# Gates, branch projections and merge computed with tokens on partitions and 512 weight columns moving, merged columns transposed afterwards

## The chip, the cores and the metric

The kernel runs on one core of one Trainium2 chip. The metric is the device time of one execution in microseconds (us). All arrays are float32 in memory. TensorE (PE in the profile) multiplies, VectorE (DVE) and ScalarE (ACT) prepare operands and empty PSUM, SyncE (SP) issues nearly all weight DMAs in the order of the program, GpSimd (POOL) issues a few small ones.

## What is computed

One transformer layer over 256 latent tokens with 256 context tokens and D_MODEL = 2048. The change touches the gates and the merge of its two branches:

```python
proj = h @ w_in[l]                       # h: 256 x 2048; columns: q, kv, u, v, gates
attn_o = _attention(q, k, v)             # 256 x 1024
sgu_o = _sgu(u, v, ...)                  # 256 x 1024
g = sigmoid(proj[..., OFF_GATE:])        # 256 x 4096
merged = g[..., :2048] * (attn_o @ w_br_attn) + g[..., 2048:] * (sgu_o @ w_br_sgu)
x_new = x + g1 * (merged @ w_out[l])
...                                      # then norm, modulation and a SwiGLU FFN
```

## The kernel before

**Products.** A float32 weight tile of 128 x 512 is split into a high part `whi` (ACT, L241) and a low part `wlo` (DVE, L242); activations are kept as high and low halves of one 128 x 512 tile (`split_to`, L290 on ACT and L291 on DVE). A product is three matmuls (`mm3`): high x high, high x low, low x high. There are two ways round. With **channels on partitions** the 128 x 128 weight tile is stationary and the 256 tokens move (`mm<-g,whi` in the profile). With **tokens on partitions** a 128 x 128 activation tile is stationary and 512 weight columns move (`mm<-whi,g`). `mm_wides` is a form of the first way: both halves of the activation move as 512 columns past `whi`, then the high half as 256 columns past `wlo`; the two halves of the PSUM bank are added afterwards (L641, L642).

**Stages.** In order: modulation vectors and the input projection in chunks of the contraction (`in_chunk`, order given by the string `ORDER`, with blocks "T" of 512 columns, tokens on partitions, and tiles "F" of 128 columns, channels on partitions); the spatial-gating branch; query, key and value up-projections; attention; branch projections and merge; output projection (`project(mg, wout, ...)`); norm; FFN. The gate columns are PE work that fills other stages: `fill_items` is a generator that yields after every 1 MB of weights, and `SGU_GATES`, `UQ_GATES` and `ATT_GATES` say how many steps are placed after which piece. What is left of it (two steps and the eight steps of the projection of the spatial branch) runs after the attention (`fill(40, MOD_RATE)`). Then the loop over `wbra` projects the attention output, multiplies by the gate (L872), adds the other branch (L873) and splits the result into the tiles `mg` (L290, L291), channels on partitions, as `project` needs them.

**Beside it.** `background(rate)` places modulation work between the steps: each item loads 512 KB of `w_mod` and adds it to an accumulator on DVE (L427); 96 items must be done before the last column block of the output projection. Raw weights have 10 buffers of 512 KB, `whi` and `wlo` 8 each, which is two 1 MB steps ahead of PE. PSUM has 4 banks `mm` and 4 `ax`. A scheduler puts the instructions of each engine in one fixed row; each engine then runs its row in order.

Of the kernel before, what the change touches and what calls it, by code (L numbers as in the profile page):

```python
# [9 lines left out]
F32R = mybir.dt.float32r  # L10
AF = mybir.ActivationFunctionType
ALU = mybir.AluOpType

P = 128
D = 2048
KT = D // P
# [17 lines left out]
OFF_KVC = Q_LORA  # L34
# [31 lines left out]
HOLD_AT = 0  # L66


NB_Q, NB_V = 1, 2
NB_T = NB_Q + NB_V  # L70
NT_U, NT_G = 8, 32
KV_COLS = KV_LORA + ROPE

NT_GE = 4
NT_F = NT_U + NT_GE

ATT_GATES = [2, 2, 2, 2, 0, 4, 0, 2]
UQ_GATES = [2, 2, 0, 0, 0, 0]
# [44 lines left out]
def block_kernel(  # L123
# [43 lines left out]
    def slot(dt=F32):  # L167
        return gp.tile([P, 512], dt, tag="g", name=f"g{uid()}")
# [4 lines left out]
    def mmbank():  # L173
        return pm.tile([P, 512], F32, tag="mm", name=f"mm{uid()}")
# [76 lines left out]
    def flat(ap, off, ncols):  # L251
        return ap[off:off + P * ncols]
# [40 lines left out]
    def hilo(t):  # L293
        return t[:, 0:256], t[:, 256:512]
# [316 lines left out]
    for o in ORDER:  # L611
        todo[o].pop(0)()

    acc_v = acc_t[NB_Q:]
    acc_u = acc[0:NT_U // 2]


    gate_a, gate_b = acc[NT_U // 2:], []
    sgo = []
    raw_gates = list(gate_a)  # L620

    def sigmoids():

# [1 line left out]
            S.activation(d, d, AF.Sigmoid)  # L625
        raw_gates.clear()

    def fill_items():
        for i in range((NT_G - NT_GE) // 2):
            d = slot()  # L630
            pair = [mmbank(), mmbank()]
            for c in range(2):
                w = W(flat(wgate, (2 * i + c) * P * WCOLS, WCOLS), WCOLS)
                for kk in range(KT // 2):
                    k = c * (KT // 2) + kk
                    mm_wides(pair, [w.cols((2 * kk + h) * P) for h in range(2)], hs[k], k == 0, k == KT - 1)
                if c == 0:
                    yield
            for h, ps in enumerate(pair):
                v = d[:, h * 256:(h + 1) * 256]  # L640
                S.activation(v, ps[:, 256:512], AF.Copy)  # L641
                V.tensor_tensor(out=v, in0=ps[:, 0:256], in1=v, op=ALU.add)  # L642
            raw_gates.append(d)
            (gate_b if i < NT_G // 4 else gate_a).append(d)
            yield

        sigmoids()
        for i in range(8):
            w = W(flat(wbrs, i * P * WCOLS, WCOLS), WCOLS)
            ps = mmbank()  # L650
            for j in range(2):
                for k in range(8):
                    mm3(ps[:, j * 256:(j + 1) * 256], w.cols((j * 8 + k) * P), hilo(sgo[k]), k == 0, k == 7)
            V.tensor_tensor(out=gate_b[i], in0=ps, in1=gate_b[i], op=ALU.mult)
            yield

    gi = fill_items()
# [205 lines left out]


    mg = []
    for i in range(8):
        w = W(flat(wbra, i * P * WCOLS, WCOLS), WCOLS)
        ps = mmbank()
        for j in range(2):
            for k in range(8):  # L870
# [3 lines left out]
        for j in range(2):  # L874
# [171 lines left out]
def _layout(inp):  # L1046
# [44 lines left out]
    for ang in (row, col):  # L1091
# [19 lines left out]
    ge = OFF_GATE + NT_GE * P  # L1111
    wg = np.concatenate([wi[:, OFF_GATE + D:], wi[:, ge:OFF_GATE + D]], axis=1)
    wg = wg.reshape(2, KT // 2, P, (NT_G - NT_GE) // 2, 2, P)
    o["wgate"] = np.concatenate([
        x for i in range((NT_G - NT_GE) // 2) for c in range(2) for x in _chunk(wg[c, :, :, i].transpose(1, 0, 2, 3))])
    blocks = np.concatenate([wi[:, :OFF_KVC], wi[:, OFF_V:OFF_GATE]], axis=1).reshape(KT, P, NB_T, 512)
    tiles = np.concatenate([wi[:, OFF_U:OFF_V], wi[:, OFF_GATE:ge]], axis=1).reshape(KT, P, NT_F, P)
    a = {"T": blocks, "F": tiles}
    o["win"] = np.concatenate([
        x for g, items in in_chunks() for x in _chunk(np.concatenate(  # L1120
# [13 lines left out]
        inp["b_spatial"][0].reshape(-1)]).reshape(-1, 512))  # L1134
    o["xN"] = np.ascontiguousarray(inp["x"][0])

    pairs = [[2 * i, 2 * i + 1] for i in range(8)]
    o["wbrs"] = _pack(inp["w_br_sgu"][0], list(range(8)), pairs)
    o["wbra"] = _pack(inp["w_br_attn"][0], list(range(8)), pairs)
# [32 lines left out]
```

## Time and profile before

| | before |
|---|---|
| median of 3 runs (lowest, highest) | 1431.43 us (1430.92, 1431.45) |
| the profiled execution's own time | 1432.35 us |
| its span, first to last instruction | 1430.5 us |
| mean granted TensorE clock | 0.997 |
| PE busy | 1403.3 us (98%) |
| DVE busy | 1009.4 us (71%) |
| ACT busy | 766.0 us (54%) |

The stages in the trace: input projection to about 220 us, spatial branch and up-projections with gates to 350, attention with gates to 487, the last gates to 498, the spatial branch's projection to 550, the attention branch's to 597, the output projection to 681, then the FFN. A busy PE row counts the pipeline's length too, so the duration of one matmul is longer than the step from its start to the next one's; where the cost of a stream of matmuls is wanted, the steps between starts are to be read.

### The profile page before, as it was taken

The page shows a single profiled execution, that of the slowest core. Times are in us where ns is not written, and L with a number is a line of the kernel's source. Part 1 is how long each engine was busy: PE and PEld are TensorE (multiplying, and loading weights), DVE is VectorE, ACT ScalarE, POOL GpSimd, SP SyncE. Part 2 cuts the span into 40 slices and gives each one's busy share as a digit, 9 for nine tenths or more (in the row PEclk, how much of TensorE's full clock was granted, in tenths as well). Part 3 has the DMA queues.
Part 4 walks back from the last instruction along what each step waited for, and adds up shares of the span by engine and source line. Part 5 has one row for each costly group of instructions (what it writes and reads, how often), then busy time and mean ns, then how long its engine had stood idle before and what let it go on. Part 6 is the DMA issues. An engine that isn't in the chain of part 4 may idle for free.

```text
span 1430.5 us, 23109 instructions
## 1 busy us (share of the span) xinstructions
PE 1403.3 (98%) x8390; PEld 1187.3 (83%) x8390; DVE 1009.4 (71%) x1748; ACT 766.0 (54%) x1438; POOL 21.9 (2%) x44
## 2 busy tenths in 40 slices
PE   6999999999999999999999999999999999999998
PEld 3787899896777799987888888888888888888887
DVE  2677687985798688999766666666666667786553
ACT  4655466565544745554666555555555554444442
POOL 0000000001100000000000000000000000000000
PEclk9999999999999999999999999999999999999999
DMA  9987876674698598898444555555555568898560
GB/s 370 359 316 294 342 277 237 241 275 146 208 355 321 166 408 294 289 402 341 161 162 153 187 191 191 186 190 187 189 191 188 192 209 303 310 374 301 197 206 32
DMA packets 104020, 355.50 MB, mean 249 GB/s; under 512 B 12504, under 2 KB 14936, under 8 KB 103904
## 3 DMA queue, kind: packets, MB, share of 16 engines
q1 hardware_dynamic: 101952, 350.30, 67.5%
q0 software_dynamic: 1952, 3.72, 1.0%
q8 instruction: 66, 1.08, 0.3%
q14 instruction: 50, 0.41, 0.1%
HBM read 351.83 MB, written 2.13 MB: 247 GB/s over the span
## 4 chain that ended last, share of the span: by engine, by line
PE 86%; DVE 6%; DMA 5%; issue 2%; ACT 2%; SPq 0%; POOL 0%; DVEq 0%; ACTq 0%; POOLq 0%
PE mm L255 80%; PE ax L255 5%; DVE wlo L242 2%; DVE acc L427 2%; DMA raw<-in_wmod_dram 1%; DMA raw<-in_win_dram 1%; DMA raw<-in_wout_dram 1%; PE ax L840 1%; DMA g<-in_rows_dram 0%; ACT whi L241 0%; DMA m_d<-g 0%; DMA sh<-m_d 0%; DVE g L837 0%; ACT g L386 0%; DMA g<-in_xT_dram 0%
## 5 line engine op out<-in xcount | busy, mean ns | idle before, releaser
L241 ACT ACTIVATE whi<-raw 128x512 fp32r<-128x512 f32 (+1 forms) x900 | 555.4, 627 | 481.8 <-PE mm L255 334.8
L242 DVE TENSOR_TENSOR wlo<-raw,whi 128x512 fp32r<-128x512 f32 (+1 forms) x900 | 603.8, 685 | 263.5 <-ACT whi L241 255.1
L255 PE MATMUL mm<-g,whi 128*128 128x512 f32 (+1 forms) x2880 | 767.9, 357 | 0.0
L255 PE MATMUL mm<-g,wlo 128*128 128x256 f32 x2368 | 505.3, 281 | 0.0
L255 PEld LDWEIGHTS mm<-g,wlo 128*128 128x128 f32 x2368 | 438.3, 189 | 78.9 <-issue 2.0
L255 PEld LDWEIGHTS mm<-g,whi 128*128 128x128 f32 x2880 | 447.9, 190 | 14.6 <-issue 8.3
L255 PE MATMUL mm<-whi,g 128*128 128x512 f32 (+1 forms) x1312 | 401.3, 385 | 1.9 <-ACT whi L241 1.2
L255 PEld LDWEIGHTS mm<-whi,g 128*128 128x128 f32 x1312 | 244.6, 189 | 53.9 <-issue 3.7
L255 PE MATMUL mm<-wlo,g 128*128 128x512 f32 (+1 forms) x656 | 251.5, 384 | 0.7 <-DVE wlo L242 0.7
L427 DVE SCALAR_TENSOR_TENSOR acc<-raw,silw,acc 128x1024 f32<-128x1024 f32 x120 | 153.4, 1279 | 20.3 <-DMA raw<-in_wmod_dram 19.7
L255 PEld LDWEIGHTS mm<-wlo,g 128*128 128x128 f32 x656 | 123.7, 189 | 25.7 <-DVE wlo L242 2.5
L561 DVE TENSOR_TENSOR g<-mm,g 128x512 f32<-128x512 f32 (+1 forms) x72 | 46.3, 654 | 23.4 <-PE mm L255 22.9
L290 ACT ACTIVATE g<-g 128x256 fp32r<-128x256 f32 x100 | 39.1, 412 | 13.9 <-DVE g L1008 8.3
L1006 DVE TENSOR_TENSOR g<-mm,g 128x256 f32<-128x256 f32 x88 | 33.3, 420 | 17.4 <-ACT g L1005 17.3
L1005 ACT ACTIVATE g<-mm 128x256 f32<-128x256 f32 x88 | 29.0, 381 | 30.9 <-PE mm L255 30.9
L291 DVE TENSOR_TENSOR g<-g,g 128x256 fp32r<-128x256 f32 x100 | 40.2, 420 | 7.1 <-ACT g L290 7.0
L255 PE MATMUL ax<-g,g 128*128 128x128 f32 (+2 forms) x224 | 42.7, 374 | 0.2 <-DVE g L702 0.2
L255 PEld LDWEIGHTS ax<-g,g 128*128 128x128 f32 (+1 forms) x224 | 26.7, 190 | 11.7 <-issue 9.2
L255 PE MATMUL ax<-raw,silw 128*32 128x256 f32 (+1 forms) x576 | 31.6, 358 | 3.7 <-DMA raw<-in_wmod_dram 3.6
L255 PEld LDWEIGHTS ax<-raw,silw 128*32 128x32 f32 x576 | 17.0, 109 | 16.3 <-DMA raw<-in_wmod_dram 5.7
L386 ACT ACTIVATE g<-g,m 128x256 f32<-128x256 f32 x32 | 17.6, 593 | 10.2 <-DVE m L375 5.8
L835 ACT ACTIVATE g<-g,nb,rq 128x512 f32<-128x512 f32 x16 | 13.0, 811 | 14.4 <-DVE nb L833 14.3
(146 smaller groups left out, 452.0 us busy)
## 6 DMA issues: line engine op xcount, KB each, us to landing
raw<-in_wmod_dram SPq DMA_DIRECT2D x192, 512.0 KB, 6.6
raw<-in_wffi_dram SPq DMA_DIRECT2D x176, 512.0 KB, 3.2
raw<-in_wffo_dram SPq DMA_DIRECT2D x88, 512.0 KB, 4.8
raw<-in_wgate_dram SPq DMA_DIRECT2D x56, 512.0 KB, 5.0
raw<-in_win_dram SPq DMA_DIRECT2D x48, 512.0 KB, 7.0
raw<-in_wout_dram SPq DMA_DIRECT2D x32, 512.0 KB, 7.6
raw<-in_wbrs_dram SPq DMA_DIRECT2D x16, 512.0 KB, 9.0
raw<-in_wbra_dram SPq DMA_DIRECT2D x16, 512.0 KB, 6.4
```

What stands on the lines that cost most here:

```text
L241: S.activation(hi[:, :e], raw[:, q:q + e], AF.Copy)
L242: V.tensor_tensor(out=lo[:, :e], in0=raw[:, q:q + e], in1=hi[:, :e].bitcast(F32), op=ALU.subtract)
L255: nc.tensor.matmul(out, lhsT, rhs, start=start, stop=stop)
L290: S.activation(dst_hi, src, AF.Copy)
L291: V.tensor_tensor(out=dst_lo, in0=src, in1=dst_hi.bitcast(F32), op=ALU.subtract)
L386: S.activation(v, v, AF.Identity, bias=m[:, 2 * jj + s:2 * jj + s + 1], scale=m[:, 2 * n + 2 * jj + s:2 * n + 1 + 2 * jj + s])
L427: V.scalar_tensor_tensor(out=acc, in0=w.raw[0], scalar=sil[:, k, 0:1], in1=acc, op0=ALU.mult, op1=ALU.add)
L561: V.tensor_tensor(out=d, in0=ps, in1=d, op=ALU.add)
L835: exp = S.activation(t, t, AF.Exp, bias=nb, scale=rq[:, col:col + 1], accum_out=sm)
L840: nc.tensor.transpose(tp[:, k * P:(k + 1) * P], t[:, k * P:(k + 1) * P], ident)
L1005: S.activation(d, ps[:, 256:512], AF.Copy)
L1006: V.tensor_tensor(out=d, in0=ps[:, 0:256], in1=d, op=ALU.add)
```

## The change

All 32 tiles of gate columns become 8 blocks of 512 columns with tokens on partitions: one in the input projection (a fourth "T" block in place of four "F" tiles), seven in `fill_items`. A block needs two PSUM banks, one for each 128 tokens, and four 1 MB steps (`quarter`), where a pair of tiles needed two banks and two steps. Both branch projections are done the same way, four blocks of two steps. The merged values now have tokens on partitions, so after each block of the attention branch eight 128 x 128 transposes on PE (L884) turn them, and `split_to` reads the turned columns from PSUM. Weights are laid out anew on the host; bytes and counts of DMAs stay.

```diff
-        for i in range((NT_G - NT_GE) // 2):
-            d = slot()
-            pair = [mmbank(), mmbank()]
...
-                    mm_wides(pair, [w.cols((2 * kk + h) * P) for h in range(2)], hs[k], k == 0, k == KT - 1)
...
-                S.activation(v, ps[:, 256:512], AF.Copy)
-                V.tensor_tensor(out=v, in0=ps[:, 0:256], in1=v, op=ALU.add)
+    def quarter(ps, src, w_d, i, c, nk):
+        w = W(flat(w_d, i * P * WCOLS, WCOLS), WCOLS)
+        for j in range(4):
+            k = 4 * c + j
+            for tt in range(2):
+                mm3(ps[tt], rows_of(src, k, tt), w.cols(j * 512, 512), k == 0, k == nk - 1)
...
+        for i in range(NB_G - NB_GE):
+            ps = [mmbank(), mmbank()]
+            for c in range(KT // 4):
+                quarter(ps, hs, wgate, i * (KT // 4) + c, c, KT)
...
+            for tt in range(2):
+                S.activation(d[tt], ps[tt], AF.Copy)
...
-        for i in range(8):
...
-                    mm3(ps[:, j * 256:(j + 1) * 256], w.cols((j * 8 + k) * P), hilo(sgo[k]), k == 0, k == 7)
-            V.tensor_tensor(out=gate_b[i], in0=ps, in1=gate_b[i], op=ALU.mult)
+        for i in range(4):
+            ps = [mmbank(), mmbank()]
+            for c in range(2):
+                quarter(ps, sgo, wbrs, 2 * i + c, c, 8)
...
     mg = []
-    for i in range(8):
...
-                mm3(ps[:, j * 256:(j + 1) * 256], w.cols((j * 8 + k) * P), hilo(ao[k]), k == 0, k == 7)
-        V.tensor_tensor(out=gate_a[i], in0=ps, in1=gate_a[i], op=ALU.mult)
-        V.tensor_tensor(out=gate_a[i], in0=gate_a[i], in1=gate_b[i], op=ALU.add)
-        for j in range(2):
-            t = slot(F32R)
-            split_to(t[:, 0:256], t[:, 256:512], gate_a[i][:, j * 256:(j + 1) * 256])
-            mg.append(t)
-        background(MOD_RATE)
+    for i in range(4):
+        ps = [mmbank(), mmbank()]
+        for c in range(2):
+            quarter(ps, ao, wbra, 2 * i + c, c, 8)
+            background(MOD_RATE)
+        for tt in range(2):
+            g = gate_a[i][tt]
+            V.tensor_tensor(out=g, in0=ps[tt], in1=g, op=ALU.mult)
+            V.tensor_tensor(out=g, in0=g, in1=gate_b[i][tt], op=ALU.add)
+        for j in range(0, 4, 2):
+            tp = auxbank()
+            for jj in range(2):
+                for tt in range(2):
+                    nc.tensor.transpose(tp[:, jj * 256 + tt * P:jj * 256 + (tt + 1) * P],
+                                        gate_a[i][tt][:, (j + jj) * P:(j + jj + 1) * P], ident)
+            for jj in range(2):
+                t = slot(F32R)
+                split_to(t[:, 0:256], t[:, 256:512], tp[:, jj * 256:(jj + 1) * 256])
+                mg.append(t)
```

PE's row before, where the third item of the `wbra` loop follows the second (`mm_6400` and `mm_6484` are their PSUM banks, `g_...` the activations):

```order
L255 MATMUL mm_6400<-g_5518,wlo_6397 128x256
L255 MATMUL mm_6400<-g_5530,whi_6396 128x256 x2
L255 MATMUL mm_6400<-g_5530,wlo_6397 128x256
L255 MATMUL mm_6484<-g_4537,whi_6466 128x256 x2
L255 MATMUL mm_6484<-g_4537,wlo_6467 128x256
L255 MATMUL mm_6484<-g_4549,whi_6466 128x256 x2
```

PE's row now, where the second block follows the first (`mm_5858` and `mm_5859` are the second block's banks, `g_167` and `g_168` the first block's merged values of tokens 0 to 127 and 128 to 255, `ax_...` the banks of the transposes):

```order
L255 MATMUL mm_5859<-whi_5862,g_4281 128x512
L255 MATMUL mm_5858<-whi_5866,g_4293 128x512
L884 MATMUL ax_5836<-cst,g_167 128x128
L884 MATMUL ax_5847<-cst,g_167 128x128
L255 MATMUL mm_5858<-wlo_5867,g_4293 128x512
L255 MATMUL mm_5858<-whi_5866,g_4293 128x512
L884 MATMUL ax_5836<-cst,g_168 128x128
L884 MATMUL ax_5836<-cst,g_167 128x128
L884 MATMUL ax_5836<-cst,g_168 128x128
L884 MATMUL ax_5847<-cst,g_168 128x128
L884 MATMUL ax_5847<-cst,g_167 128x128
L884 MATMUL ax_5847<-cst,g_168 128x128
```

PE's row had nothing between two items that needs DVE's merge; now the merged values of the block just finished are read after seven matmuls of the next block (ten after the third and the fourth block).

DVE's row before, around the multiplication of the third item:

```order
L242 TENSOR_TENSOR wlo_6631<-raw_6624,whi_6630 128x512
L872 TENSOR_TENSOR g_4594<-mm_6484,g_4594 128x512
L242 TENSOR_TENSOR wlo_6637<-raw_6634,whi_6636 128x512
L873 TENSOR_TENSOR g_4594<-g_4594,g_3108 128x512
L242 TENSOR_TENSOR wlo_6641<-raw_6634,whi_6640 128x512
L291 TENSOR_TENSOR g_6535<-g_4594,g_6535 128x256
```

DVE's row now, after the first block:

```order
L242 TENSOR_TENSOR wlo_5910<-raw_5907,whi_5909 128x512
L427 SCALAR_TENSOR_TENSOR acc_5825<-raw_5904,silw,acc_5825 128x1024
L242 TENSOR_TENSOR wlo_5914<-raw_5907,whi_5913 128x512
L877 TENSOR_TENSOR g_167<-mm_5716,g_167 128x512
L877 TENSOR_TENSOR g_168<-mm_5717,g_168 128x512
L878 TENSOR_TENSOR g_167<-g_167,g_2926 128x512
L878 TENSOR_TENSOR g_168<-g_168,g_2927 128x512
L242 TENSOR_TENSOR wlo_5920<-raw_5917,whi_5919 128x512
L242 TENSOR_TENSOR wlo_5924<-raw_5917,whi_5923 128x512
L291 TENSOR_TENSOR g_5841<-ax_5836,g_5841 128x256
```

The four multiplications and additions of a block stand together, behind an accumulation (L427) and the split of weights, and the splits of the merged values come after PE's transposes. In front of the fourth block's four stand the two additions of a bias row (L413), which wait for a DMA of `in_rows`.

## Rows read from the trace of the kernel before

**Rows 1.** The page: busy time of each engine, and PE's busy tenths in 40 slices.
```profile
PE 1403.3 (98%) x8390; PEld 1187.3 (83%) x8390; DVE 1009.4 (71%) x1748; ACT 766.0 (54%) x1438; POOL 21.9 (2%) x44
PE   6999999999999999999999999999999999999998
```

**Rows 2.** PE's waits: who waited for whom, us in total, times, longest.
```profile
PE ax L840 <- DVE g L837: 4.8, 10, 1.2
...
PE mm L255 <- DVE wlo L242: 0.7, 2, 0.6
```

**Rows 3.** Busy time by stretch: stretch, length, each engine, clock, DMA share, GB/s.
```profile
120.00:220.00 100.00, 99.41 (x764) 87.04 (x763) 76.10 (x162) 56.66 (x119) 0.00 (x0) 1.00 0.76 286
400.00:487.00 87.00, 83.58 (x482) 63.33 (x481) 69.04 (x127) 46.61 (x93) 5.90 (x11) 1.00 0.74 267
498.00:550.00 52.00, 52.00 (x440) 51.76 (x439) 41.88 (x59) 23.56 (x40) 0.00 (x0) 1.00 0.96 378
550.00:597.00 47.00, 47.00 (x372) 45.62 (x365) 44.81 (x71) 24.81 (x49) 3.06 (x6) 1.00 0.85 297
597.00:660.00 63.00, 63.00 (x281) 50.89 (x280) 62.79 (x87) 31.19 (x57) 3.06 (x6) 1.00 0.99 379
```

**Rows 4.** The chain that ended last, 545 to 720 us (start, us, what).
```profile
579.40 0.03 DVE g L872
...
586.00 6.96 DMA g<-in_rows_dram
...
628.82 7.43 DMA raw<-in_wout_dram
...
668.88 12.10 PE mm L255 x52
```

**Rows 5.** PE's timeline, a pair of gate tiles (start, us, what, count).
```profile
488.76 0.63 PE L255 MATMUL mm<-g,whi 128*128 128x512 f32 x2
...
489.23 0.39 PE L255 MATMUL mm<-g,wlo 128*128 128x256 f32 x2
...
489.46 0.63 PE L255 MATMUL mm<-g,whi 128*128 128x512 f32 x2
```

**Rows 6.** PE's timeline, projection of the spatial branch.
```profile
499.25 0.40 PE L255 MATMUL mm<-g,whi 128*128 128x256 f32 x2
...
499.61 0.40 PE L255 MATMUL mm<-g,whi 128*128 128x256 f32 x2
```

**Rows 7.** PE's timeline, output projection.
```profile
597.32 0.62 PE L255 MATMUL mm<-whi,g 128*128 128x512 f32 x2
...
598.00 0.62 PE L255 MATMUL mm<-whi,g 128*128 128x512 f32 x2
```

**Rows 8.** PE's timeline, eight transposes of the query latents amid matmuls.
```profile
205.26 1.11 PE L512 MATMUL ax<-cst,g 128*128 128x128 f32 x8
206.13 0.47 PE L255 MATMUL mm<-whi,g 128*128 128x512 f32 x1
206.44 0.40 PE L255 MATMUL mm<-wlo,g 128*128 128x512 f32 x1
```

**Rows 9.** Groups of instructions by form: count, busy us, mean ns of one, idle before.
```profile
L840 PE MATMUL ax<-cst,g 128*128 128x128 f32 x64 | 10.1, 281 | 5.0 <-DVE g L837 4.8
```

**Rows 10.** DVE's timeline, attention branch's projection.
```profile
584.28 1.27 DVE L427 SCALAR_TENSOR_TENSOR acc<-raw,silw,acc 128x1024 f32<-128x1024 f32 x1
585.48 0.68 DVE L872 TENSOR_TENSOR g<-mm,g 128x512 f32<-128x512 f32 x1
...
587.88 0.75 DVE L291 TENSOR_TENSOR g<-g,g 128x256 fp32r<-128x256 f32 x2
588.55 1.28 DVE L242 TENSOR_TENSOR wlo<-raw,whi 128x512 fp32r<-128x512 f32 x2
589.76 1.27 DVE L427 SCALAR_TENSOR_TENSOR acc<-raw,silw,acc 128x1024 f32<-128x1024 f32 x1
593.05 1.36 DVE L413 TENSOR_TENSOR g<-g,g 128x512 f32<-128x512 f32 x2 [2.02 <-DMA g<-in_rows_dram]
```

More of the change, by code (lines that the diff above doesn't have):

```diff
@@ L66 @@
 HOLD_AT = 0
-NB_Q, NB_V = 1, 2
-NB_T = NB_Q + NB_V
-NT_U, NT_G = 8, 32
+NB_Q, NB_V, NB_G = 1, 2, 8
+NT_U = 8
 KV_COLS = KV_LORA + ROPE
-NT_GE = 4
-NT_F = NT_U + NT_GE
+NB_GE = 1
+NB_T = NB_Q + NB_V + NB_GE
+NT_F = NT_U
 ATT_GATES = [2, 2, 2, 2, 0, 4, 0, 2]
@@ L612, in block_kernel @@
         todo[o].pop(0)()
-    acc_v = acc_t[NB_Q:]
+    acc_v = acc_t[NB_Q:NB_Q + NB_V]
     acc_u = acc[0:NT_U // 2]
-    gate_a, gate_b = acc[NT_U // 2:], []
+    gate_a, gate_b = acc_t[NB_Q + NB_V:], []
     sgo = []
-    raw_gates = list(gate_a)
+    raw_gates = [t for g in gate_a for t in g]
     def sigmoids():
@@ L626, in sigmoids @@
         raw_gates.clear()
-    def fill_items():
-        for i in range((NT_G - NT_GE) // 2):
-            d = slot()
-            pair = [mmbank(), mmbank()]
+    def quarter(ps, src, w_d, i, c, nk):
[4 more added lines that the diff above has]
+                mm3(ps[tt], rows_of(src, k, tt), w.cols(j * 512, 512), k == 0, k == nk - 1)
+    def fill_items():
+        for i in range(NB_G - NB_GE):
+            ps = [mmbank(), mmbank()]
+            for c in range(KT // 4):
+                quarter(ps, hs, wgate, i * (KT // 4) + c, c, KT)
+                if c < KT // 4 - 1:
+                    yield
+            d = [slot(), slot()]
+            for tt in range(2):
+                S.activation(d[tt], ps[tt], AF.Copy)
+            raw_gates.extend(d)
+            (gate_b if i < NB_G // 2 else gate_a).append(d)
+            yield
+        sigmoids()
+        for i in range(4):
+            ps = [mmbank(), mmbank()]
             for c in range(2):
-                w = W(flat(wgate, (2 * i + c) * P * WCOLS, WCOLS), WCOLS)
-                for kk in range(KT // 2):
-                    k = c * (KT // 2) + kk
-                    mm_wides(pair, [w.cols((2 * kk + h) * P) for h in range(2)], hs[k], k == 0, k == KT - 1)
+                quarter(ps, sgo, wbrs, 2 * i + c, c, 8)
                 if c == 0:
                     yield
-            for h, ps in enumerate(pair):
-                v = d[:, h * 256:(h + 1) * 256]
-                S.activation(v, ps[:, 256:512], AF.Copy)
-                V.tensor_tensor(out=v, in0=ps[:, 0:256], in1=v, op=ALU.add)
[L643 to L647, printed above, removed]
-        for i in range(8):
-            w = W(flat(wbrs, i * P * WCOLS, WCOLS), WCOLS)
-            ps = mmbank()
-            for j in range(2):
-                for k in range(8):
-                    mm3(ps[:, j * 256:(j + 1) * 256], w.cols((j * 8 + k) * P), hilo(sgo[k]), k == 0, k == 7)
-            V.tensor_tensor(out=gate_b[i], in0=ps, in1=gate_b[i], op=ALU.mult)
+            for tt in range(2):
+                V.tensor_tensor(out=gate_b[i][tt], in0=ps[tt], in1=gate_b[i][tt], op=ALU.mult)
             yield
@@ L865, in block_kernel @@
     mg = []
-    for i in range(8):
[L867 to L870, printed above, removed]
-                mm3(ps[:, j * 256:(j + 1) * 256], w.cols((j * 8 + k) * P), hilo(ao[k]), k == 0, k == 7)
-        V.tensor_tensor(out=gate_a[i], in0=ps, in1=gate_a[i], op=ALU.mult)
-        V.tensor_tensor(out=gate_a[i], in0=gate_a[i], in1=gate_b[i], op=ALU.add)
-        for j in range(2):
-            t = slot(F32R)
-            split_to(t[:, 0:256], t[:, 256:512], gate_a[i][:, j * 256:(j + 1) * 256])
-            mg.append(t)
-        background(MOD_RATE)
+    for i in range(4):
[10 more added lines that the diff above has]
+            for jj in range(2):
+                for tt in range(2):
+                    nc.tensor.transpose(tp[:, jj * 256 + tt * P:jj * 256 + (tt + 1) * P],
[4 more added lines that the diff above has]
+                mg.append(t)
     def project(src, w_d, cb, nk, rate, last=1):
@@ L1110, in _layout @@
     o["wkv"] = np.concatenate([x for ks in kv_groups() for x in _chunk(kv[ks].transpose(1, 0, 2), 3 * KV_COLS)])
[L1111 to L1117, printed above, removed]
+    ge = OFF_GATE + NB_GE * 512
+    o["wgate"] = _nat(np.concatenate([wi[:, OFF_GATE + D:], wi[:, ge:OFF_GATE + D]], axis=1))
+    blocks = np.concatenate([wi[:, :OFF_KVC], wi[:, OFF_V:ge]], axis=1).reshape(KT, P, NB_T, 512)
+    tiles = wi[:, OFF_U:OFF_V].reshape(KT, P, NT_F, P)
     a = {"T": blocks, "F": tiles}
@@ L1135, in _layout @@
     o["xN"] = np.ascontiguousarray(inp["x"][0])
-    pairs = [[2 * i, 2 * i + 1] for i in range(8)]
-    o["wbrs"] = _pack(inp["w_br_sgu"][0], list(range(8)), pairs)
-    o["wbra"] = _pack(inp["w_br_attn"][0], list(range(8)), pairs)
+    o["wbrs"] = _nat(inp["w_br_sgu"][0])
+    o["wbra"] = _nat(inp["w_br_attn"][0])
     o["wout"] = _nat(inp["w_out"][0])
```

## The prediction

> **What bounds the kernel now.** I read the busy times and the 40 slices first. PE is busy 98% of the span, and only the first and the last slice are below nine tenths [rows 1], so the engine to watch is PE, and what the change is worth is first of all what PE's own stream becomes shorter by. A busy share can hide short stalls, so I read next PE's list of waits: the largest item is 4.8 us in the attention, where transposes wait for the softmax, and waits for a split weight come to 0.7 us in all [rows 2]. Then the stretches [rows 3]: from 498 to 660 us PE is busy all the time, but there two others come close. DVE is busy 44.81 of 47 us in the projection of the attention branch and 62.79 of 63 in the output projection, and the DMA engines run at a share of 0.96 and 0.99 around it. The chain that ended last says the same: from 579.40 to 668.88 us it doesn't run over PE but over DVE and DMAs (a bias row from `in_rows`, 6.96 us; a piece of `w_out`, 7.43 us), and PE comes back only at 668.88 [rows 4]. So before 550 us PE alone sets the pace; from there to 669 us PE and DVE with the DMAs are tied.
>
> **What a stream of matmuls costs.** Steps between starts, not durations. One pair of gate tiles (256 weight columns) for one k takes 489.46 - 488.76 = 0.70 us for four matmuls [rows 5], so 1.40 us for 512 columns and one k. Channels on partitions with `mm3` take 499.61 - 499.25 = 0.36 us for 128 columns [rows 6], so 1.44 us for 512. Tokens on partitions take 598.00 - 597.32 = 0.68 us for 512 columns and 128 tokens [rows 7], so 1.36 us for all 256, or 0.2267 us for a matmul. The moving columns are the same, 3072, in all three; there are 8, 12 and 6 matmuls for them, and what is saved is what each matmul costs beside its columns.
>
> **The change part by part.**
> Gates in `fill_items`: 7 blocks x 16 k x (1.40 - 1.36) = 4.5 us less on PE. Half of it lies among the attention, where PE is busy 83.58 of 87 us [rows 3] and fills gaps of the softmax; there a shorter filler may leave a longer gap. I take 4.0, with 2.2 (all of the attention's half lost) and 4.5 as ends. DVE and ACT lose the additions of the two PSUM halves, which is no part of the sum, since PE sets the pace there.
> Gate block in the input projection: 16 k x (1.44 - 1.36) = 1.3 us. The last two of six groups of k (8 of 16) lie where PE is busy 99.41 of 100 us [rows 3] and count fully, 0.6 us; the earlier ones lie partly where PE waits for data. I take 0.9, ends 0.6 and 1.3.
> Projection of the spatial branch: 4 blocks x 8 k x 0.08 = 2.6 us. That stretch has the DMA engines at 0.96 [rows 3], but PE is 52.00 of 52 there: two steps of split weights cover it. If the cover is gone the 2.6 us are lost.
> Projection of the attention branch: the same 2.6 us.
> Transposes: 4 blocks x 8 = 32. Eight of them took 206.13 - 205.26 = 0.87 us amid such matmuls, and the matmul behind them took 0.31 instead of 0.23 to its successor [rows 8], so 0.95 us for eight and 3.8 us for 32. The ends are 32 x 0.109 = 3.5 and, if every one cost its whole duration of 0.281 [rows 9], 32 x 0.281 = 9.0. I take 3.8, since these rows stand between the same kind of matmuls.
> New waits at the transposes: this is what the trace of before doesn't show. PE's row now asks for the merged values seven matmuls after the end of a block, 7 x 0.2267 = 1.6 us. DVE must have done two multiplications and one addition by then; at 0.60 us each (the second half of [rows 10]: two splits of 512 columns in 589.76 - 588.55 = 1.21) that is 1.8 us, and the first can begin while the second bank's last three matmuls, 0.7 us, still run. So it fits, but only just, and only if DVE isn't behind. DVE's work in a block of two steps is 8 splits x 0.60, 4 of merge x 0.60, 4 small splits x 0.335 (588.55 - 587.88 for two [rows 10]) and 2.8 accumulations x 1.20 (585.48 - 584.28 [rows 10]): 4.8 + 2.4 + 1.3 + 3.4 = 11.9 us. PE's is 48 x 0.2267 + 0.95 = 11.8. DVE has no room, and its small splits now wait for the transposes. Queued behind a waiting transpose is all of PE; before, the merge could be late by many microseconds, since PE needed `mg` only in the output projection. The nearest row is the attention's transposes that wait for DVE: 4.8 us over 16 groups of four, 0.3 each, 1.2 at most [rows 2]; for four groups 1.2, and 4.8 at most. In front of the fourth block's merge stand besides the two bias additions that waited 2.02 us for their row [rows 10], which PE didn't feel before. Ends 0 and 4.8 + 2.0 = 6.8; I take 1.5, near the mean wait, since the scheduler left DVE's merge just enough time.
> Unchanged: bytes, DMAs and their order, ACT's and DVE's splits of weights, the FFN. The sigmoids are 16 tiles as before; the pair of banks that a block holds for four steps leaves two for the query projection, whose banks are emptied one after the other.
>
> Sum: -4.0 - 0.9 - 2.6 - 2.6 + 3.8 + 1.5 = -4.8 us. Against the profiled execution's own 1432.35 us (span 1430.5 and 1.85 around it) that is 1427.6; this execution lies 0.92 us above the median of the runs, so against the median, 1431.43, it is **1426.6 us**.
>
> A rule weighed: the Trainium skill (TensorE: Matmul & The Clock Gate, Part 4: PE-mode transpose) gives about 275 ns for one 128 x 128 transpose in a kernel, most of it latency. By the page's figure, taken as a step, the term would be 8.8 us in place of 3.8 and the sum about 0.2 us slower. The trace agrees with it as a duration, 281 ns [rows 9], and not as a step, 0.87 us for eight [rows 8].
>
> **The rivals.**
> *No net gain, the tie decides.* From 579 to 669 us the chain runs over DVE and DMAs [rows 4] at 379 GB/s and a DMA share of 0.99 [rows 3]. If that chain can't begin earlier, all that PE gains ahead of it waits at its end: 1431.4, with 1429 to 1433.5 around it. For it: the tie; PE's step through a block of the attention branch gets longer (11.8 us, for 32 x 0.36 = 11.5), so DVE's list doesn't get shorter. Against it: the chain begins with a PE result at 579.40 [rows 4], and buffers that PE empties earlier are filled earlier. Chance 0.22.
> *Slower: DVE paces the merge.* Place: the four groups of transposes. If DVE comes to each block's four operations a full queue late, say two accumulations and a split, 2 x 1.20 + 0.60 = 3.0 us [rows 10], PE stands still 4 x 3 = 12 us, and the time is 1431.4 - 6.3 + 12 = 1437. It decides the sign from 6.3 us of waiting on, 1.6 for each block, and shows as slower by over 0.2% from 9.2 us on, 2.3 for each. For it: DVE at 44.81 of 47 us and the accumulation in front of the merge, which waits for its own DMA. Against it: when PE stands, DVE catches up, so the lateness doesn't add up from block to block. Chance 0.09.
> *Transposes at full price*, 9.0 us in place of 3.8 [rows 9]: 1431.4 - 10.1 + 9.0 + 1.5 = 1431.8. For it: they come in groups of two and six, and at each change of kind the pipeline could run empty. Against it: eight in 0.87 us [rows 8]. Chance 0.03.
> *All goes well*: no wait at the transposes, 4.5, 1.3 and twice 2.6 gained for 3.5: 1431.4 - 7.5 = 1424. Chance 0.06.
>
> **How the numbers follow.** The forecast has 0.60 and by its ends reaches from 1424 to 1428.5; "no net gain" 0.22, slower 0.09, full price 0.03, all well 0.06. A range from 1423.0 to 1431.5 holds the forecast, the good case and about half of the two cases of no gain, some 0.79. A measurement of this kernel can tell about 0.2%, 2.9 us, from no change: faster means under 1428.6, slower over 1434.3. Faster: 0.60 + 0.06 = 0.66; same: 0.22 + 0.03 = 0.25; slower: 0.09.
>
> **What would show it.** In the profile after, the step of a gate block for one k should be 1.36 us and the same in both projections; the 32 transposes should step by about 0.11 to 0.12 us. The last gates should end about 5 us earlier (near 493) and the spatial branch's projection about 7.5 us earlier (near 542). A wait of PE for DVE at L884 should stand in the list of waits with 1 to 3 us; over 6 us would make the slower rival. From there on the output projection should end 4 to 5 us earlier than 681 and the FFN take as long as before. If the spatial branch's projection ends 7 us earlier and the FFN begins at the old time, the tie decided. If steps of 0.70 and 0.36 us stay, the arithmetic of steps was wrong.

## The result: slower, by a wait in the attention that the prediction didn't name

| | before | changed |
|---|---|---|
| median of 4 runs (lowest, highest) | 1431.36 us (1430.92, 1431.45) | 1443.36 us (1440.55, 1444.28) |
| ratio to before, 95% interval | | 1.0081 (1.0069 to 1.0093) |
| profiled execution, span | 1430.5 us | 1441.5 us |

The change costs 12.0 us, 0.8%, where 4.8 us of gain were forecast, and the time lies above the range. PE's busy time hardly moves, 1403.3 us [rows 1] to 1403.0, while the span grows by 11.0. So PE stands still more, and the slices say where (the page of the changed kernel: busy time and PE's busy tenths, as in [rows 1]):

```profile
PE 1403.0 (97%) x7718; PEld 1156.1 (80%) x7718; DVE 1000.8 (69%) x1720; ACT 766.4 (53%) x1424; POOL 21.7 (2%) x44
PE   6999999999988999999999999999999999999998
```

Slices 12 and 13 (396 to 468 us) are the attention. PE's waits in the changed kernel, to be held against [rows 2] (L844 and L841 are what L840 and L837 were):

```profile
PE ax L844 <- DVE g L841: 11.4, 7, 5.4
...
PE ax L255 <- DVE g L706: 2.1, 2, 1.0
...
PE ax L884 <- DVE g L878: 1.4, 1, 1.4
```

The wait for the softmax has gone from 4.8 us in ten pieces, none over 1.2, to 11.4 in seven, one of 5.4. The new transposes at L884, on which the prediction spent its worry, wait 1.4 us.

To see where each part came out, I read off PE's timeline when the same work begins in both kernels:

| PE begins | before | changed | later by | piece up to here longer by |
|---|---|---|---|---|
| first work behind the input projection | 222.11 | 221.13 | -1.0 | -1.0 |
| sums for the query norm (128x4) | 326.36 | 326.20 | -0.2 | +0.8 |
| first scores of the attention | 347.60 | 348.99 | +1.4 | +1.6 |
| last gates, behind the attention | 486.58 | 495.96 | +9.4 | +8.0 |
| first modulation sums (`acc`) | 549.73 | 556.00 | +6.3 | -3.1 |
| second modulation sums | 612.60 | 622.03 | +9.4 | +3.2 |
| FFN | 693.93 | 704.11 | +10.2 | +0.8 |

A minus sign means earlier, or shorter. From there on the first 489 us of the FFN are equal (488.86 and 488.85); the whole piece from the FFN's start to the end takes 736.5 to 737.4 us in the profiled executions of all kernels here, so the last 0.8 us of the 11.0 is scatter. Eight of the ten microseconds are lost inside the attention.

**What DVE does there.** One operation of DVE that nobody needs in the attention stands in the middle of the softmax: the bias add of the MLP's shift vector (`sh2`, 8 columns, 0.17 us), which is first read at 696 us. The modulation work makes it like this:

```python
for q in range(4):                                   # POOL: sums to memory (L450)
    nc.gpsimd.dma_start(m_d[q:q + 1, :], e[32 * q:32 * q + 1, 0:256])
nc.gpsimd.dma_start(sh2[:, b * 8:(b + 1) * 8], ...)  # POOL: and back, turned (L453)
due.append(lambda b=b: shift(b))                     # DVE: L408, issued at k == MOD2_DUE of the next item
```

DVE's timeline of the changed kernel (start, duration, what, and in brackets how long DVE had stood and for whom), first around 395 us, then around 438:

```profile
395.89 0.17 DVE L408 TENSOR_TENSOR sh<-sh,prm 128x8 f32<-128x8 f32 x1 [3.13 <-DMA sh<-m_d]
396.01 0.69 DVE L833 CUSTOM_DVE_ANT_0 g<-ax,rst 128x512 f32<-128x512 f32 x1
...
397.82 0.15 DVE L837 TENSOR_TENSOR nb<-mx,nrq 128x1 f32<-128x1 f32 x1
...
399.14 0.16 DVE L840 RECIPROCAL sm<-sm 128x1 f32<-128x1 f32 x1
...
400.46 0.48 DVE L841 TENSOR_SCALAR g<-g,sm 128x512 f32<-128x512 f32 x1
...
433.83 0.15 DVE L837 TENSOR_TENSOR nb<-mx,nrq 128x1 f32<-128x1 f32 x1
438.88 0.17 DVE L408 TENSOR_TENSOR sh<-sh,prm 128x8 f32<-128x8 f32 x1 [4.90 <-DMA sh<-m_d]
...
440.16 0.16 DVE L840 RECIPROCAL sm<-sm 128x1 f32<-128x1 f32 x1
...
440.83 0.48 DVE L841 TENSOR_SCALAR g<-g,sm 128x512 f32<-128x512 f32 x1
```

And DVE's timeline of the kernel before at the same two places (there L833 is the exponent's bias, behind the maximum, L836 the reciprocal, L837 the scaling):

```profile
393.47 0.15 DVE L833 TENSOR_TENSOR nb<-mx,nrq 128x1 f32<-128x1 f32 x1
...
394.74 0.15 DVE L836 RECIPROCAL sm<-sm 128x1 f32<-128x1 f32 x1
394.81 0.15 DVE L408 TENSOR_TENSOR sh<-sh,prm 128x8 f32<-128x8 f32 x1
...
436.54 0.15 DVE L833 TENSOR_TENSOR nb<-mx,nrq 128x1 f32<-128x1 f32 x1
437.96 0.17 DVE L408 TENSOR_TENSOR sh<-sh,prm 128x8 f32<-128x8 f32 x1 [1.27 <-DMA sh<-m_d]
```

Before, the first L408 stood behind the maximum, the exponent's bias and the reciprocal of its softmax (the attention's fifth) and found its data there; now it stands ahead of all three (L833, L837, L840) and DVE stops for 3.13 us. At the second place it stands behind the bias both times, but of the ninth softmax where it was the tenth, and DVE reaches it 4.9 us before its data where it was 1.3. Behind L408 in DVE's row lie the reciprocal and the scaling, and for these PE waits. The chain of waits of the changed kernel names every link:

```profile
426.07 0.39 ACT g L447
...
428.22 5.37 DMA m_d<-g
...
434.25 4.61 DMA sh<-m_d
...
438.88 0.04 DVE sh L408
...
440.83 0.49 DVE g L841
...
441.45 1.09 PE ax L844 x4
```

From ACT's copy of the sums to L408 it is 12.8 us, 10.0 of them two small transfers one behind the other. The chain of waits of the kernel before ran over the same links already, with little room to spare (PE's wait at its end, 441.17 us, was 1.20 us, the longest of [rows 2]):

```profile
424.91 6.39 DMA m_d<-g
...
431.96 5.98 DMA sh<-m_d
...
437.96 0.06 DVE sh L408
```

**And a second price.** After the stand of 5.4 us PE is slow for a while. Busy time by stretch in the changed kernel (columns as in [rows 3]), then PE's timeline (count `x2` for two matmuls):

```profile
401.00:404.00 3.00, 2.91 (x15) 2.51 (x16) 3.00 (x7) 1.69 (x3) 0.00 (x0) 1.00 0.89 328
...
436.00:441.40 5.40, 0.03 (x1) 0.00 (x0) 2.52 (x6) 0.47 (x1) 0.00 (x0) 0.88 0.31 96
441.40:447.20 5.80, 5.75 (x16) 4.74 (x17) 4.75 (x8) 1.23 (x2) 0.00 (x0) 0.52 0.77 268
447.20:450.00 2.80, 2.80 (x14) 2.25 (x12) 1.41 (x5) 2.03 (x5) 0.00 (x0) 1.00 0.90 268
```

```profile
401.09 0.63 PE L844 MATMUL ax<-cst,g 128*128 128x128 f32 x4 [3.46 <-DVE g L841]
...
441.45 1.09 PE L844 MATMUL ax<-cst,g 128*128 128x128 f32 x4 [5.42 <-DVE g L841]
...
442.77 1.05 PE L255 MATMUL mm<-whi,g 128*128 128x512 f32 x2
...
444.05 1.05 PE L255 MATMUL mm<-whi,g 128*128 128x512 f32 x2
...
448.16 0.62 PE L255 MATMUL mm<-whi,g 128*128 128x512 f32 x2
...
448.84 0.62 PE L255 MATMUL mm<-whi,g 128*128 128x512 f32 x2
```

Three matmuls take 444.05 - 442.77 = 1.28 us there and 448.84 - 448.16 = 0.68 us a little later; the granted clock is 0.52 and then 1.00, its lower and its upper level (1.2 and 2.4 GHz). The twelve matmuls from 442.19 to 447.25 take 5.06 us in place of 12 x 0.2267 = 2.72, so 2.3 us are lost beside the wait. The clock fell while PE still stood (0.88 in the mean from 436.00 to 441.40). After the first stand, 3.46 us until 401.09, it stayed at 1.00.

Theory 1, then: the loss is L408's place in DVE's row, 8 us of waits and 2.3 us of slow clock, and has nothing to do with how a gate is computed. The rival, theory 2: the new gate step, 24 matmuls where it was 32 (the expectations call this half the instructions), is too short a filler, and the softmax would come late wherever L408 stands. Theory 3: the loss belongs to the projections and transposes.

### The profile page after: what moved, and what is told of

Its sections match the earlier page's. It is cut to its first block, busy times and chain, and to the rows that moved or that the text cites. A ratio compares the mean times of both kernels' runs of the same rounds, so it can differ in the third digit from the quotient of the medians.

```text
span 1441.5 us, 21687 instructions
## 1 busy us (share of the span) xinstructions
PE 1403.0 (97%) x7718; PEld 1156.1 (80%) x7718; DVE 1000.8 (69%) x1720; ACT 766.4 (53%) x1424; POOL 21.7 (2%) x44
## 4 chain that ended last, share of the span: by engine, by line
PE 65%; DVE 3%; DMA 2%; issue 1%; ACT 0%; POOL 0%; DVEq 0%; POOLq 0%; ACTq 0%
PE mm L255 63%; PE ax L255 2%; DVE acc L427 1%; DMA raw<-in_wmod_dram 1%; DVE wlo L242 1%; DMA g<-in_rows_dram 1%; PE ax L844 0%; DMA m_d<-g 0%; DMA sh<-m_d 0%; PE ax L884 0%; DVE g L936 0%; DVE g L916 0%; DVE g L413 0%; DVE g L841 0%; ACT whi L241 0%
## 5 line engine op out<-in xcount | busy, mean ns | idle before, releaser
L255 PE MATMUL mm<-whi,g 128*128 128x512 f32 (+1 forms) x2080 | 643.9, 388 | 1.2 <-ACT whi L241 0.8
L255 PE MATMUL mm<-g,whi 128*128 128x512 f32 (+1 forms) x1792 | 510.7, 374 | 0.0
L255 PEld LDWEIGHTS mm<-whi,g 128*128 128x128 f32 x2080 | 389.7, 189 | 87.6 <-issue 9.5
L255 PE MATMUL mm<-wlo,g 128*128 128x512 f32 (+1 forms) x1040 | 403.8, 389 | 1.5 <-DVE wlo L242 1.5
L255 PEld LDWEIGHTS mm<-g,wlo 128*128 128x128 f32 x1600 | 295.0, 188 | 60.1 <-issue 1.3
L255 PE MATMUL mm<-g,wlo 128*128 128x256 f32 (+1 forms) x1600 | 327.5, 281 | 0.0
L255 PEld LDWEIGHTS mm<-g,whi 128*128 128x128 f32 x1792 | 279.2, 189 | 9.1 <-issue 2.9
L255 PEld LDWEIGHTS mm<-wlo,g 128*128 128x128 f32 x1040 | 196.5, 189 | 42.8 <-DVE wlo L242 3.9
L427 DVE SCALAR_TENSOR_TENSOR acc<-raw,silw,acc 128x1024 f32<-128x1024 f32 x120 | 153.7, 1281 | 20.0 <-DMA raw<-in_wmod_dram 19.5
L291 DVE TENSOR_TENSOR g<-g,g 128x256 fp32r<-128x256 f32 x84 | 34.3, 422 | 6.0 <-ACT g L290 5.6
L844 PE MATMUL ax<-cst,g 128*128 128x128 f32 x64 | 10.6, 290 | 12.2 <-DVE g L841 11.4
```

Source lines behind the costliest of these rows:

```text
L255: nc.tensor.matmul(out, lhsT, rhs, start=start, stop=stop)
L291: V.tensor_tensor(out=dst_lo, in0=src, in1=dst_hi.bitcast(F32), op=ALU.subtract)
L427: V.scalar_tensor_tensor(out=acc, in0=w.raw[0], scalar=sil[:, k, 0:1], in1=acc, op0=ALU.mult, op1=ALU.add)
L844: nc.tensor.transpose(tp[:, k * P:(k + 1) * P], t[:, k * P:(k + 1) * P], ident)
```

## The experiments

### L408 moved out of the attention: e1_late, and its control e2_before_late

```diff
-                    due.append(lambda b=b: shift(b))
+                    shifts.append(lambda b=b: shift(b))
...
-            V.tensor_tensor(out=xv, in0=t, in1=xv, op=ALU.add)
+            xo = V.tensor_tensor(out=xv, in0=t, in1=xv, op=ALU.add)
...
+        if cb == 1:
+            with tc.issue_after(xo.ins):
+                for f in shifts:
+                    f()
```

> The changed kernel with one edit: the two bias adds of the MLP's shift (VectorE, L408, 0.17 us each) are issued behind the second block of the output projection instead of inside the attention, so that VectorE's row never stands at them while their DMA is under way. Theory 1 (the loss is VectorE's row: in the changed kernel L408 stands in front of softmax operations and waits 3.1 and 4.9 us for a DMA, PE then waits 3.5 and 5.4 us for the scaled rows): the L844 <- L841 wait falls from 11.4 us to 5 or less, no stretch at a granted clock of 0.66 near 442 us, and the time is 1443.4 - 8 = 1435 (1433 to 1437). Theory 2 (a gate step of half the instructions is too short to cover a softmax, wherever L408 stands): the waits move to other softmax operations, the time stays within 1441 to 1444.

> The kernel before with the same edit (both L408 adds behind the second block of the output projection). Theory 1: only 1.3 us of wait goes, and PE's wait for it is covered in part: 1430 to 1431.5. Theory 2: no change, 1431.4. It is the control that late adds are not a gain of their own of 8 us.

Measured: e1_late 1435.57 us (1433.43 to 1437.95), ratio to before 1.0028 (1.0017 to 1.0038); e2_before_late 1435.36 us, 1.0023 (1.0013 to 1.0033). The first is as theory 1 said, 7.8 us faster than the changed kernel; theory 2 falls. The control missed: the same edit made the old kernel 3.5 us slower, where it was to do nothing. In its trace PE stands 2.76 us for a weight split until 665.99 us, and the granted clock is 0.50 from 667.3 to 670.6. PE's waits in e1_late show both, and DVE's timeline the reason:

```profile
PE mm L255 <- DVE most L930: 3.3, 1, 3.3
PE ax L846 <- DVE g L843: 3.3, 7, 0.7
```

```profile
656.74 0.68 DVE L242 TENSOR_TENSOR wlo<-raw,whi 128x512 fp32r<-128x512 f32 x1
657.34 0.69 DVE L918 TENSOR_TENSOR g<-g,g 128x512 f32<-128x512 f32 x1
...
661.54 1.89 DVE L918 TENSOR_TENSOR g<-g,g 128x512 f32<-128x512 f32 x3
...
663.47 0.69 DVE L242 TENSOR_TENSOR wlo<-raw,whi 128x512 fp32r<-128x512 f32 x1
```

The softmax's wait is gone (11.4 us to 3.3, less than the 4.8 of the kernel before). But in the last block of the output projection ten operations for the second norm and its scale (L415, L418, L918, 0.60 us each) now stand between two weight splits, and PE waits 3.3 us for the second, at 664 us. How many splits stand between the first sum for the norm (`most`) and these ten operations decides the wait: five in the kernel before (0.2 us), four in the changed kernel (0.9 us at 677.71, most of the last +0.8 of the table), three in e4_proj_only below (1.6), two in e2_before_late (2.8), one here (3.3). My edit had moved a second piece of DVE's row without meaning to.

### One number in the kernel before: e5_before_early

```diff
-                    if k == MOD2_DUE:
+                    if k == {(1, 1): 4, (0, 0): 3}.get((s, b), MOD2_DUE):
```

> The kernel before with one number changed: the two L408 adds are issued earlier in the pieces that carry them, so that in VectorE's row they stand ahead of the softmax as they do in the changed kernel. By the rows of before its first DMA lands at 393.3 us and VectorE would be at L408 at 389.5: a wait of some 3.5 us; the second waits some 2 us instead of 1.3. Theory 1: the old gates pay for it too, PE's wait for the scaled softmax rows goes from 4.8 to 7 to 10 us and the time to 1433.5 to 1436.5. Theory 2 (only the short gate steps are at fault): 1431 to 1432.5.

Measured: 1443.91 us (1443.23 to 1444.96), ratio 1.0090 (1.0076 to 1.0104). The old gates, with L408 three or four steps earlier, lose as much as the whole change: the short filler isn't needed for it. The size missed my expectation by 7 us (its upper end was 1436.5), for two reasons that its trace shows. The waits are longer than I worked out from before, 9.3 us in two for L408 (4.07 and 5.26), and PE waits for the softmax (the first line is from PE's waits, the others are busy time by stretch)

```profile
PE ax L840 <- DVE g L837: 12.6, 9, 5.5
```

```profile
400.00:405.00 5.00, 5.00 (x17) 4.42 (x18) 3.86 (x8) 2.05 (x4) 0.00 (x0) 0.50 0.94 342
...
445.00:450.00 5.00, 5.00 (x19) 4.42 (x19) 3.54 (x8) 2.02 (x4) 0.00 (x0) 0.50 0.93 331
```

and after both stands, 4.30 and 5.46 us, PE runs the next 5 us at 0.50 of its clock; I had priced the waits alone.

### The halves of the change: e3_gates_only and e4_proj_only

In the first the gates alone are made with tokens on partitions (wider blocks, `quarter`), in the second only projections, merge and transposes. In both the merge multiplies numbers that don't belong together, so the outputs are not the layer's.

> Only the gates are made with tokens on partitions; the projections and the merge stay as before (the merged products pair numbers of other layouts, so the output is not the model's; the work and its order are those of the gates part alone). Theory 1 and theory 2: the loss of the attention comes with the gates alone, +8 to +9 against before, 1439 to 1441, with L408 waiting some 8 us as in the changed kernel. Rival theory 3 (the projections and the transposes behind the attention carry the loss): 1429 to 1432.

> Only the two branch projections, the merge and the transposes are changed; the gates stay with channels on partitions (the merged products pair numbers of other layouts, so the output is not the model's). VectorE's row in the attention is that of before. Theory 1 and theory 2: the attention costs what it did; the second projection gains 2.9 us and the first stage with the transposes loses 3.1 us: 1430 to 1433. Theory 3: 1438 to 1442.

Measured: e3_gates_only 1440.12 us (1435.91 to 1444.71), ratio 1.0063 (1.0038 to 1.0087); L408 stands where it does in the changed kernel, waits 6.1 us in all, and PE 9.5 us for the softmax. e4_proj_only 1431.17 us, 0.9994 (0.9985 to 1.0003); L408 stands where it did in the kernel before and doesn't wait. Theory 3 falls: the loss comes with the gates, because with them DVE's row in the attention is laid out anew. The wide scatter of the first would fit a wait for transfers that land now earlier, now later; only one of its executions was profiled, so this isn't shown.

### Both places in DVE's row repaired: e6_late_spread, and its control e8_before_late_spread

```diff
 (as e1_late, and)
-    def project(src, w_d, cb, nk, rate, last=1):
+    def project(src, w_d, cb, nk, rate, last=1, hook=None):
...
+            if hook and c == 1:
+                hook()
...
-            for i in range(3):
-                for tt in range(2):
-                    scaled(i, tt)
...
-        ps = project(mg, wout, cb, KT, MOD_RATE if cb < 3 else 0.0, 2 if cb == 3 else 1)
+        ps = project(mg, wout, cb, KT, MOD_RATE if cb < 3 else 0.0, 2 if cb == 3 else 1,
+                     (lambda: [scaled(i, tt) for i in range(3) for tt in range(2)]) if cb == 3 else None)
```

> The changed kernel with L408 late as in the first experiment, and with the six products of x and the second norm's scale issued one chunk later in the last block of the output projection. In the first experiment ten such VectorE operations in a row stood ahead of the chunk's weight splits, and PE waited 3.3 us there (664 us); here two splits stand between them. Theory 1 with this second place: that wait goes to under 0.5 us and the time is 1435.6 - 3 = 1432.5 (1431 to 1434). If the remaining loss of the first experiment is not that wait: 1434.5 to 1436.

> The kernel before with L408 late and the six products one chunk later: the control of the sixth label. Theory 1: the 2.8 us wait that the late add caused at 666 us in the second experiment goes, and with it all that this edit cost: 1430 to 1432. The sixth label minus this one is then what the change itself is worth without the two waits: by the traces (-0.9 transposes of T, -3.1 first projection, +3.1 second projection with transposes, +1.4 key sums) about 0 to +1 us.

Measured: e6_late_spread 1429.65 us (1429.18 to 1432.17), ratio 0.9991 (0.9982 to 1.0000); e8_before_late_spread 1431.29 us (1430.59 to 1432.23), 1.0000 (0.9991 to 1.0008). The repaired old kernel is the old kernel again, and the repaired new one is 13.7 us faster than the change as made and 1.6 us faster than the repaired old one; ten of its eleven runs lie below the lowest of e8's. It came out 1.4 us below the range that I expected. By the profiled executions e6 gains 4.2 us on e1 (spans of 1432.1 and 1427.9), near the wait of 3.3; why the medians differ by 5.9 isn't shown. The two traces give the change's own worth, piece by piece, with DVE's row alike: to the first scores +1.1; attention 136.17 us against 138.00, -1.8; last gates and first projection 60.04 against 63.15, -3.1; from there to the second modulation sums 65.82 against 62.87, +3.0; the rest 0.0. That is 0.9 in these two executions, where the medians give 1.6.

### What is left to gain: e7_late_spread_turn, e12_late_spread_turn_only, e11_before_late_spread_keys

Two more new costs stand in the changed kernel's PE row. The transposes of the last merged block wait for the merge, and the merge for a bias row, as the prediction had it; PE's timeline and then DVE's:

```profile
601.51 0.41 PE L884 MATMUL ax<-cst,g 128*128 128x128 f32 x2 [1.36 <-DVE g L878]
```

```profile
598.19 1.37 DVE L413 TENSOR_TENSOR g<-g,g 128x512 f32<-128x512 f32 x2 [1.30 <-DMA g<-in_rows_dram]
```

And the sums of the key squares (`kss`, on four groups of 32 columns of the array) are strewn singly among other matmuls; PE's timeline of the changed kernel, a lone one (two records to a sum, so `x2`) and a group of three:

```profile
331.04 1.05 PE L255 MATMUL ax<-g,unit 128*32 128x512 f32 x2
332.02 0.49 PE L255 MATMUL mm<-g,whi 128*128 128x512 f32 x1
...
341.25 1.06 PE L255 MATMUL ax<-g,unit 128*32 128x512 f32 x6
342.24 0.49 PE L255 MATMUL mm<-whi,g 128*128 128x512 f32 x1
```

One alone takes 0.98 us to the next instruction, three together 0.99. Before, the eight came in three lone or paired places of 0.98 and one group of 1.78 (340.24 to 342.02), 4.7 us; in the changed kernel in five lone ones and one group of three, 5.9 us. That is most of the +1.6 us ahead of the first scores. The Trainium skill (TensorE: Matmul & The Clock Gate, Part 3: Packing small matmuls) has it that column tiles on different column groups run at the same time; this trace agrees, three for the price of one; the group of four took 1.78 us.

The edits: the transposes of block i are issued behind the first half of block i+1's projection, and the first four sums behind head 5 (e7; e12 has the first edit alone, e11 is e8 with the second alone).

```diff
+            if turn:
+                turn_block(turn.pop())
             background(MOD_RATE)
...
-        if h % 4 == 3:
+        if h in (5, 7):
+            j = h == 7
```

> The kernel of the sixth label with two more moves in PE's row: the transposes of a merged block are issued behind the first half of the next block's projection (so they run eight in a row and don't wait for VectorE's products), and the first four 32-column sums of the key squares are issued behind head 5 instead of head 3, so that three of them run side by side. Priced by rows of the changed kernel: the waits at L884 of 1.4 us go, the lone 32-column matmuls of 0.98 us become fewer, -1 us: 1430 (1428 to 1431.5). If neither was on the path: as the sixth label, 1432.5.

> The sixth label with only the transposes moved behind the first half of the next block's projection, the key sums left at head 3: it splits the 3.0 us by which the seventh is faster than the sixth. By the wait that it takes away (1.2 us at L886) and its fuller groups: 1428.2 (1427.3 to 1429). If the key sums carry all: 1429.6.

> The kernel before with both repairs and with the first four 32-column sums of the key squares behind head 5 (as in the seventh): the control for the seventh. In before two of the four stood side by side already, so it has less to gain: -0.5, 1430.8 (1430 to 1431.5). If the seventh's 3 us came from the key sums and not from the change: 1428.3 to 1429.5.

Measured: e7_late_spread_turn 1426.63 us (1424.56 to 1428.09), ratio 0.9967 (0.9955 to 0.9979); e12_late_spread_turn_only 1427.99 us, 0.9977 (0.9968 to 0.9986); e11_before_late_spread_keys 1430.17 us, 0.9990 (0.9982 to 0.9999). e7 is below the range that I expected, the other two are inside theirs. The wait at the transposes is gone from e7's list, and eight run in one group between matmuls:

```profile
566.29 1.04 PE L878 MATMUL ax<-cst,g 128*128 128x128 f32 x8
567.08 0.48 PE L255 MATMUL mm<-whi,g 128*128 128x512 f32 x1
```

So e7 is faster than both kernels: 4.7 us faster than the one before, 16.7 than the change as made, and 3.5 us faster than the old kernel with the edits that it can share. Of its gain over e6 the transposes' place gives 1.7 and the key sums 1.4 by the medians. In the traces of e6 and e7 it is 1.3 (65.82 to 64.53 us between the modulation sums) and 2.3 (22.79 to 20.47 from the query norm to the first scores), so this split is rough.

### The halves once more, with DVE's row repaired: e9_gates_spread and e10_proj_spread

The kernels of the third and fourth experiment with the edits of e6 (outputs again not the layer's).

> Only the gates changed, as in the third experiment, with the two repairs of the sixth (L408 late, the six products one chunk later); the merged products again pair numbers of other layouts. It is to be held against the eighth label (the kernel before with both repairs). If the new gates are worth what the traces of the sixth and the eighth show up to the end of the attention: -0.75, with two gate steps behind it -0.3, so 1 us less than the eighth: 1430.3 (1429.3 to 1431.3). If the prediction's -4.9 for the gates and T's block holds once the waits are away: 1426.4.

> Only projections, merge and transposes changed, as in the fourth experiment, with the same two repairs; held against the eighth label. By the traces the first projection gains 2.6 to 3.1 us and the second with its transposes loses as much: 1431 (1430.3 to 1432). If the prediction's -2.6 -2.6 +3.8 +1.5 holds: 1431.4; if the transposes were hidden as the waits of the second projection are: 1428.

Measured: 1429.71 us (1428.67 to 1432.93), ratio 0.9990 (0.9981 to 0.9999), and 1429.68 us (1429.19 to 1432.21), 0.9990 (0.9981 to 0.9999). Each half is 1.6 us faster than e8. The gates alone are worth 1.6 us, not the 4.9 of the prediction. The projections came out 0.6 us below the range that I expected. The two don't add up, since together in e6 they give 1.6 and not 3.2, and the traces show most of the reason. Between the first and the second modulation sums e9 takes 62.86 us, as e8 does, and e10 64.39, 1.5 more, but e6 65.82, 3.0 more. In e6 DVE stands 1.10 us for the bias row ahead of the fourth block's merge and PE 1.18 us for the merged values behind it; in e10 the same additions find their row, and PE's list has no wait at the transposes. So 1.2 of the 1.6 us is a wait that only the two halves together bring. Why the row comes too late there isn't shown, and the rest is within the scatter between executions.

## Why the prediction was wrong, step by step

**The step that failed** is the gates' term. It read the stretch from 400 to 487 us as PE filling gaps of the softmax, allowed that "a shorter filler may leave a longer gap", and set the worst case at "all of the attention's half lost", 2.2 us. That was no bound, and that "PE sets the pace there" was wrong: for 8 us of the changed kernel's attention DVE set it, standing at L408 for a transfer. The change writes the gates anew, and with them the scheduler lays out DVE's row of the attention anew; what else stands in that row, and what each of its operations waits for, was not looked at. L408 and its 1.27 us wait were in the trace of before, inside a softmax, directly behind its bias. The prediction followed the chain of waits only from 545 us on [rows 4] and concluded that before 550 us PE alone sets the pace; from 424.91 to 441.17 us the same chain ran over the two transfers and L408. The price was 146.97 - 136.17 = 10.8 us, the attention of the changed kernel against that of e6. The table shows 8.0 of it, since 1.8 us of gain and the 1.0 us that L408 had cost in the kernel before (138.98 us there, 138.00 in e8) stand against it.

A second part of the miss stays when this one is repaired: e6 is 1.6 us faster than e8, not 4.8. It lies ahead of the attention: e6 reaches the first scores 1.1 us later than e8, where the forecast's terms gave 2.8 us earlier (0.9 for T's block, 1.9 for twelve gate steps).

**The size of the gates' gain** was right where nothing stood in the way. In the attention e6 gains 1.8 us on e8, where I had taken 1.8 (4.0 less 2.2). Ahead of the attention it was wrong: the twelve gate steps there should have given 12 x 0.16 = 1.9 us, but PE waits 2.1 us for DVE at L706, in the spatial gating, which it didn't before (0.2 at that line), and then pays 1.2 us more for the key sums. Both are the same kind of step as the failed one: PE's and DVE's rows changed beside the edit. By these terms the two pieces of the table up to the first scores should be 1.2 us longer; they are 2.4, and the other 1.2 I can't assign.

**T's block**: forecast 0.9, with 1.3 at most; 1.0 at the end of the input projection in the two executions of the table. Such a pair says little: that point lies between 219.65 and 221.13 us in the seven profiled executions with the new block and between 221.48 and 222.60 in the seven without it. The means, 220.2 and 221.9, are 1.7 apart, so the term was too small.

**The first projection**: forecast 2.6, and 0.3 for the two gate steps ahead of it and 0.3 for the start of the second projection that lies in the same piece; 3.1 measured. The steps of 0.68 us for 512 columns and 128 tokens held wherever the granted clock was 1.00, so the arithmetic of [rows 5 to 7] was right.

**The transposes**: forecast 0.95 us for eight. In PE's timeline of the changed kernel:

```profile
563.78 0.41 PE L884 MATMUL ax<-cst,g 128*128 128x128 f32 x2
563.95 0.48 PE L255 MATMUL mm<-wlo,g 128*128 128x512 f32 x1
...
564.50 0.82 PE L884 MATMUL ax<-cst,g 128*128 128x128 f32 x6
565.07 0.48 PE L255 MATMUL mm<-whi,g 128*128 128x512 f32 x1
565.38 0.40 PE L255 MATMUL mm<-wlo,g 128*128 128x512 f32 x1
```

0.17 + 0.57 = 0.74 us, and 0.08 more for the matmul behind each group (0.31 to its successor), so 0.90 and 3.6 in all. The Trainium skill's 275 ns for one (TensorE: Matmul & The Clock Gate, Part 4: PE-mode transpose) holds as its duration, 273 ns in the median here, and not as its step.

**The waits at L884**: forecast 1.5, measured 1.4, at the fourth block and behind the bias row, as the prediction had put it. With -2.3 for 28 steps of the second projection, 3.6 and 1.4 the piece should be 2.7 us longer; it is 3.2, and 0.5 I can't assign.

**The rivals.** "Slower: DVE paces the merge" had the right engine and the right kind of mechanism, PE standing for a late DVE, but at the wrong place: L884 waited 1.4 us where that rival needed over 6.3. "No net gain, the tie decides" isn't what happened either: in e6 the FFN begins 0.9 us earlier than in e8, and in e7 3.6 us. "Transposes at full price" falls with the 3.6 us above, and "all goes well" with the waits. That e7's 1426.6 us equals the number forecast for the change is chance: it contains the key sums and the transposes' place, which the forecast didn't.

What stays open: why the scheduler, given wider gate blocks, puts L408 ahead of the first softmax. e5 shows that the place is enough to cost 12 us and e3 that the gates' rewriting brings it, but no run varied the scheduler itself. Nor is it shown why PE waits at L706 now; this wait wasn't repaired in any run.

## What to carry to other kernels

When a change rewrites filler work around a latency-bound stage, list what else stands in the rows of the engines that the stage waits for, above all operations that wait for a DMA, and price each one standing in front of the stage; a small operation that nobody needs soon belongs behind a late one, by an explicit order. Then compare the new kernel with the old one only after giving both the same repair, or the change is judged by where the scheduler happened to put something else. A control that applies the repair to the old kernel also catches what the repair itself moves, as e2 did.

## What the runs showed of the hardware

A stand of PE can cost more than its length: after 4.3 and 5.5 us (e5) and 5.4 us (changed kernel) the granted clock stood at 0.50 to 0.52 over the next five microseconds and the matmul's step was 0.43 us in place of 0.227, 2.3 us more in the changed kernel. Which stands do this the length alone doesn't tell: after 3.46 us (changed kernel) and 3.29 us (e1, until 664.22) the clock stayed at 1.00, and after 2.76 us (e2, until 665.99) it was 0.50 from 667.3 to 670.6. A round trip of 4 KB through memory on POOL's queue took 10.0 us in the changed kernel (the second L408's), 5.4 out and 4.6 back, beside weight loads that had the DMA engines at a share of 0.88 from 426 to 434 us; the same trip in the kernel before took 6.4 out and 6.0 back.
